# The projection's 101 scratch stores begun by GpSimd instead of the sync engine, in a one-core decoder layer

## The chip, the cores and the metric

The kernel runs on one core of a Trainium2 chip. The metric is the device time of one execution in microseconds; before the change it is 1848.69 us, the median of three runs (1846.27 to 1848.75). Profiled executions are shown in us from the start of the span. The engines are TensorE (PE, and PEld for its weight loads), VectorE (DVE), ScalarE (ACT), GpSimd (POOL) and the sync engine (SP), which computes nothing and begins DMAs.

## The reference, cut to what matters

One layer of a hybrid decoder is computed for a prompt of 2048 tokens and for a group of 8 x 8 sample tokens with the same weights. A normalised input `h` is projected once, and the columns of the projection feed four mixers and a gate:

```
h = rms_norm(x, norm_pre)
proj = jnp.einsum('btd,de->bte', h, w_in)
q = proj[..., OFF_AQ:OFF_AK]; k = proj[..., OFF_AK:OFF_AV]; v = proj[..., OFF_AV:OFF_B]
xb = proj[..., OFF_B:OFF_C]; pc = proj[..., OFF_C:OFF_D]; u = proj[..., OFF_D:OFF_G]; gate = proj[..., OFF_G:]
...
oa = attend(q, k, v, lam)                  # differential attention: w = p0 - lam * p1; w @ v
ob, new_h = rglru(xc, lru_h, ...)          # from xb
oc, new_shift, new_S = rwkv7_mix(pc, ...)
od, new_ssm = s5_mix(u, ...)
o = jnp.concatenate([oa, ob, oc, od], axis=-1) * jax.nn.silu(gate)
y = x + rms_norm(jnp.einsum('bte,ed->btd', o, w_out), norm_post)
```

The change concerns `pc` (the RWKV group's five projections), `u` (the S5 group's) and `gate`, which the kernel computes while it runs the prompt's attention.

## The kernel before

`w_in` is 28 column blocks of 128; a group `g` is two of them. The first stage (to 286 us of the span) normalises the input and projects groups 0 to 3: queries, keys, values and the input of the RG-LRU group, which it also runs. The second stage, 286 to 1008 us, is the one that the change touches. Two lists of work run in it together:

- `attn_prompt` and `attn_rows` (L317, L350): for each of 4 heads and 16 blocks of 128 queries, a row of attention over pieces of 512 keys; 64 rows, 160 pieces. Per piece: the scores `s` (L363, TensorE), their maxima `a_mx` (L367, VectorE), the exponentials `a_e` (L371, ScalarE). Per row, the factors `a_al` (L376 or L387, VectorE). Then per piece the second half of `a_e` is scaled on GpSimd (L391), both halves are joined on VectorE (L392), cast to fp16 as the first half of `a_w` on ScalarE (L395), the remainder of the cast is written as the second half of `a_w` on GpSimd (L396), the sync engine begins a DMA transpose of `a_w` into `a_wt` (L399), and TensorE multiplies `a_wt` by the values into `pv` (L403, L404). `a_w` and `a_wt` have four buffers each.
- `proj_rest` (L583): the 10 other groups of the projection (`FILL`), each 2 column blocks x 5 blocks of tokens (four of 512 and one of 64), 100 accumulations `acc` of 24 matmuls (L206). Each `acc` is evicted into `pst` (three buffers) by ScalarE and VectorE: for `pc` by L624, L626 and L631, for the gate `sg` by L640 to L642, for `u` by L606 on ScalarE alone. Then `pst` is stored to scratch in DRAM: `pc` at L634 (50 stores), `sg` at L643 (40), `u` at L608 (10), and once `shift` at L636. A store of 512 columns is 128 rows of 2 KB; one of `u` is 128 x 8 runs (64 elements each, 8 in the short block). Later stages read `pc`, `u` and `sg`.

The paced order (`paced`, L1783) ties the projection's matmuls to anchors in the attention, so that both lists end together. In the same stage the output weights are halved into fp16 pairs (`w`, L1501 to L1503) and stored (L1504), and the sync engine loads `kh` and `qh` (L330, L335).

The order on each engine is made by the framework's scheduler when the program is built. On the chip each engine and each queue works in that order: an instruction that waits for a semaphore holds up all that stand behind it on its engine. The sync engine's list in this stage is the 160 transposes, the 101 stores, the loads of `kh` and `qh` and the weights' stores.

The last stage, from 1008 us, holds the sample group's attention, S5, RWKV and the output projection.

Of the kernel before, what the change touches and what calls it, by code (L numbers as in the profile page):

```python
# [53 lines left out]
class Part:  # L54
# [528 lines left out]
    def proj_rest(self, groups, wpool, pool, psum, after, aside=iter(())):  # L583


        nc = self.nc
        st_q = nc.sync
        for g in groups:
            for m in range(2):
                w16, un = self.load_w(2 * g + m, wpool)  # L590
# [1391 lines left out]
```

## Time and profile before

| | us |
|---|---|
| median of three runs | 1848.69 |
| the profiled execution | 1857.33 |
| its span | 1855.5 |
| first stage, 0 to 286 | 286 |
| second stage, 286 to 1008 | 722 |
| the rest | 847.5 |
| TensorE busy in the span | 1505.9 (81%) |
| VectorE busy | 1415.4 (76%) |
| ScalarE busy | 902.6 (49%) |
| GpSimd busy | 717.9 (39%) |

The span runs from the first to the last instruction of the program; the profiled execution's own time is 1.8 us longer. The busy time of an engine is that of its instructions alone; a DMA that the sync engine begins is not counted as busy, while one that GpSimd begins stands among its instructions. A wait is put down to the instruction whose semaphore came last. Shares of busy time are averages over stages with different limits, so the table of stretches is read beside them.

### The profile page before, as it was taken

How to read it: one execution, taken by the hardware profiler on the slowest of the kernel's cores; microseconds unless marked ns; L12 is line 12 of the kernel's file. 1: busy time of each engine (PE TensorE's matmuls, PEld its weight loads, DVE VectorE, ACT ScalarE, POOL GpSimd, SP SyncE). 2: the span in 40 equal slices, each digit the busy share in tenths (PEclk: the TensorE clock that was granted, in tenths of full speed). 3: DMA queues.
4: the chain of work that ended last, by engine and by line, in shares of the span. 5: the costliest groups of instructions: out<-in, count | busy, mean ns of one | idle time of the engine just before them, and what ended most of it. 6: DMA issues, size and time to landing. Idle time of an engine off the chain costs nothing.

```text
span 1855.5 us, 32909 instructions
## 1 busy us (share of the span) xinstructions
PE 1505.9 (81%) x10956; PEld 846.6 (46%) x10956; DVE 1415.4 (76%) x4439; ACT 902.6 (49%) x2211; POOL 717.9 (39%) x807
## 2 busy tenths in 40 slices
PE   5889878788878878888895799856777978888887
PEld 2445644344434434444442355545544544544443
DVE  7797638867888897898786765367787886988975
ACT  3445645555655665666773222243334444444443
POOL 3441312343434553563444444253323433334322
PEclk9999998899989998999897798966687878889889
DMA  4422134655545655473445986655223333233221
GB/s 148 128 87 92 35 109 109 151 117 128 110 117 132 140 150 129 115 162 94 86 105 139 270 268 204 193 170 165 75 66 85 106 90 105 82 91 96 65 85 59
DMA packets 300894, 225.31 MB, mean 121 GB/s; under 512 B 192530, under 2 KB 248564, under 8 KB 300212
## 3 DMA queue, kind: packets, MB, share of 16 engines
q1 hardware_dynamic: 288388, 184.85, 37.5%
q10 hardware_dynamic: 8496, 24.76, 4.6%
q0 software_dynamic: 3840, 13.61, 2.7%
q8 instruction: 86, 1.41, 0.3%
q14 instruction: 84, 0.69, 0.1%
HBM read 130.04 MB, written 53.24 MB: 99 GB/s over the span
## 4 chain that ended last, share of the span: by engine, by line
DVE 29%; PE 18%; DMA 14%; issue 12%; POOL 8%; ACT 4%; SPq 1%; ACTq 0%; POOLq 0%; DVEq 0%
DMA r_zr<-zd 6%; PE acc L206 4%; POOL a_w L396 4%; PE acc L1585 4%; POOL a_e L391 3%; DVE a_mx L367 3%; DMA a_wt<-a_w 2%; DVE a_e L392 2%; DVE r_x16w L1263 2%; DVE r_x L1264 2%; PE ss L512 2%; DMA zd<-r_de 2%; DMA kv<-in_ckv 1%; DVE r_W L1178 1%; ACT a_e L371 1%
## 5 line engine op out<-in xcount | busy, mean ns | idle before, releaser
L206 PE MATMUL acc<-hT,w 128*128 128x512 f16 (+1 forms) x3120 | 636.1, 356 | 39.1 <-DVE shf L628 11.9
L206 PEld LDWEIGHTS <-w 128*128 128x128 f16 x3120 | 271.1, 101 | 341.6 <-issue 70.7
L371 ACT ACTIVATE a_e<-s,a_mx,sig 128x512 f32<-128x512 f32 (+3 forms) x320 | 225.3, 713 | 111.0 <-DVE a_mx L368 88.5
L1585 PE MATMUL acc<-wo,o_h 128*128 128x512 f16 (+1 forms) x816 | 226.6, 424 | 3.5 <-DVE o_h L1563 2.1
L391 POOL TENSOR_SCALAR a_e<-a_e,a_al 128x512 f32<-128x512 f32 (+3 forms) x160 | 115.0, 734 | 287.2 <-DVE a_al L387 232.4
L396 POOL TENSOR_TENSOR a_w<-a_e,a_w 128x512 f16<-128x512 f32 (+3 forms) x160 | 180.2, 1142 | 105.0 <-ACT a_w L395 104.9
L367 DVE TENSOR_REDUCE a_mx<-s 128x1 f32<-128x512 f32 (+3 forms) x320 | 184.2, 601 | 30.7 <-PE s L363 16.5
L392 DVE SCALAR_TENSOR_TENSOR a_e<-a_e,a_al 128x512 f32<-128x512 f32 (+3 forms) x160 | 138.5, 884 | 14.4 <-POOL a_e L391 14.2
L363 PE MATMUL s<-kh,qh 128*128 128x512 f16 (+3 forms) x320 | 101.0, 358 | 40.6 <-ACT a_e L371 36.1
L1585 PEld LDWEIGHTS <-o_h 128*128 128x128 f16 (+1 forms) x816 | 77.5, 106 | 99.4 <-issue 29.3
L403 PE MATMUL pv<-vtok,a_wt 128*128 128x128 f16 x544 | 68.9, 229 | 63.7 <-DMA a_wt<-a_w 52.6
L395 ACT CAST a_w<-a_e 128x512 f16<-128x512 f32 (+3 forms) x160 | 85.7, 558 | 63.6 <-DVE a_e L392 61.9
L1263 DVE TENSOR_TENSOR r_x16w<-r_zr,r_x 128x60 f32<-128x60 f32 (+18 forms) x255 | 59.3, 233 | 54.7 <-DMA r_zr<-zd 51.8
L403 PEld LDWEIGHTS <-a_wt 128*128 128x128 f16 x544 | 51.4, 102 | 88.1 <-DMA a_wt<-a_w 76.3
L1600 POOL TENSOR_TENSOR o_x<-o_y,o_x 128x512 f32<-128x512 f32 (+1 forms) x33 | 48.9, 1496 | 105.6 <-DVE o_y L1598 72.5
L170 POOL TENSOR_TENSOR hT<-hf,hT 128x512 f16<-128x512 f32 (+1 forms) x36 | 36.7, 1026 | 88.5 <-ACT hT L168 86.1
L404 PE MATMUL pv<-vtok,a_wt 128*128 128x64 f16 x544 | 64.9, 200 | 0.0
L371 ACT ACTIVATION_READ_ACCUMULATOR a_e<-s,a_mx,sig 128x1 f32 x320 | 64.2, 201 | 0.0
L1264 DVE TENSOR_TENSOR r_x<-r_x,r_x16w 128x60 f32<-128x60 f32 (+18 forms) x255 | 59.9, 235 | 2.9
L512 PE MATMUL ss<-kv,qbd 128*32 128x256 f32 x256 | 52.7, 415 | 7.9 <-DMA kv<-in_ckv 7.9
L368 DVE TENSOR_SCALAR a_mx<-a_mx,sig 128x2 f32<-128x2 f32 x160 | 58.0, 369 | 0.5
L1365 POOL TENSOR_TENSOR r_sd<-r_Z,r_Dp 64x128 f32<-64x128 f32 x64 | 30.1, 470 | 70.0 <-DVE r_Z L1373 63.5
(545 smaller groups left out, 3201.7 us busy)
## 6 DMA issues: line engine op xcount, KB each, us to landing
kv<-in_ckv SPq DMA_DIRECT2D x128, 256.0 KB
w<-in_w_in ACTq DMA_DIRECT2D x20, 512.0 KB
pc<-pst SPq DMA_DIRECT2D x40, 256.0 KB
xw<-in_xT SPq DMA_DIRECT2D x16, 512.0 KB
w<-in_w_out ACTq DMA_DIRECT2D x16, 512.0 KB
sg<-pst SPq DMA_DIRECT2D x32, 256.0 KB
r_X<-pc SPq DMA_DIRECT2D x16, 512.0 KB
r_zr<-zd SPq DMA_DIRECT2D x16, 512.0 KB
```

The costliest lines, as they stand in the source:

```text
L206: self.nc.tensor.matmul(acc[:, :n], w16[:, k, a, :], h[:, k, e, :], start=(c == 0), stop=(c == 3 * KT - 1))
L363: ins = nc.tensor.matmul(s[:, :kn], q[:, c], kh[:, c, k0:k0 + kn], start=True, stop=True)
L367: nc.vector.tensor_reduce(mx[:, p, c:c + 1], s[:, :kn], axis=AX.X, op=ALU.max, negate=True)
L371: nc.scalar.activation(e[:, :kn], s[:, :kn], AF.Exp, scale=sig, bias=mx[:, p, c:c + 1], accum_out=l[:, p, c:c + 1])
L391: nc.gpsimd.tensor_scalar(e1[:, :kn], e1[:, :kn], al[:, p, 1:2], 0.0, op0=ALU.mult, op1=ALU.add)
L392: nc.vector.scalar_tensor_tensor(e0[:, :kn], e0[:, :kn], al[:, p, 0:1], e1[:, :kn], op0=ALU.mult, op1=ALU.add)
L396: nc.gpsimd.tensor_tensor(w[:, kn:], e0[:, :kn], w[:, :kn], op=ALU.subtract)
L403: ins = nc.tensor.matmul(pv[:, :P], wt[:, j], v, start=kt == 0, stop=kt == qb, skip_group_check=True)
L512: ins = nc.tensor.matmul(sp[g:g + 32, 256 * j:min(256 * j + 256, n)], self.qbd[:, m, s].rearrange("p a q -> p (a q)"), rhs, start=True, st ...
L1263: XV.tensor_tensor(w[:, :, :m], zr[:, k, :, k + 1:], x[:, :, k:k + 1].to_broadcast([P, nu, m]), op=ALU.mult)
L1264: XV.tensor_tensor(x[:, :, k + 1:], x[:, :, k + 1:], w[:, :, :m], op=ALU.add)
L1585: nc.tensor.matmul(a[:n].rearrange("p (c n) -> p c n", c=4), h[:, k, e], self.wo[:, 4 * g:4 * g + 4, k, f, :], start=c == 0, stop=c == 3 * ...
```

## The change

The queue that begins the stores of `proj_rest` is GpSimd's instead of the sync engine's. All three store lines and the one of `shift` use it, 101 DMAs. Nothing else in the source changes; where the instructions stand is drawn anew by the scheduler.

```diff
@@ -584,7 +584,7 @@ proj_rest
         nc = self.nc
-        st_q = nc.sync
+        st_q = nc.gpsimd
         for g in groups:
```

On the sync engine, at some 540 us of the span, the stores of three `pst` stood between transposes. `a_wt` is the transpose of the `a_w` that is named behind the arrow. Before:

```order
L399 DMA_TRANSPOSE a_wt_4851<-a_w_4848 128x8x128
L634 DMA pc_1197<-pst_9632 128x512
L399 DMA_TRANSPOSE a_wt_4922<-a_w_4919 128x8x128
L634 DMA pc_1197<-pst_9664 128x512
L634 DMA pc_1197<-pst_9695 128x64
L399 DMA_TRANSPOSE a_wt_4937<-a_w_4934 128x8x128
L399 DMA_TRANSPOSE a_wt_4952<-a_w_4949 128x2x128
```

And now:

```order
L399 DMA_TRANSPOSE a_wt_4851<-a_w_4848 128x8x128
L399 DMA_TRANSPOSE a_wt_4922<-a_w_4919 128x8x128
L399 DMA_TRANSPOSE a_wt_4937<-a_w_4934 128x8x128
L1504 DMA wod_8487<-w16_9913 128x2048
L399 DMA_TRANSPOSE a_wt_4952<-a_w_4949 128x2x128
```

The three stores are gone from this queue; the order of the transposes is kept.

On GpSimd at the same place, `a_w` of a piece and the scaling of the next row's `a_e` stood with only the weights' steps (`w32`, `w16`) between them. Before:

```order
L396 TENSOR_TENSOR a_w_4848<-a_e_4817,a_w_4848 128x512
L391 TENSOR_SCALAR a_e_4881<-a_e_4881,a_al_4871 128x512
L391 TENSOR_SCALAR a_e_4892<-a_e_4892,a_al_4871 128x512
L391 TENSOR_SCALAR a_e_4905<-a_e_4905,a_al_4871 128x128
L396 TENSOR_TENSOR a_w_4919<-a_e_4879,a_w_4919 128x512
L1502 TENSOR_SCALAR w32_9911<-w32_9911,wun_8489 128x1024
L396 TENSOR_TENSOR a_w_4934<-a_e_4890,a_w_4934 128x512
L396 TENSOR_TENSOR a_w_4949<-a_e_4903,a_w_4949 128x128
L1503 TENSOR_TENSOR w16_9913<-w32_9911,w16_9913 128x8x128
L391 TENSOR_SCALAR a_e_4973<-a_e_4973,a_al_4963 128x512
```

And now:

```order
L396 TENSOR_TENSOR a_w_4848<-a_e_4817,a_w_4848 128x512
L634 DMA pc_1197<-pst_9632 128x512
L391 TENSOR_SCALAR a_e_4881<-a_e_4881,a_al_4871 128x512
L391 TENSOR_SCALAR a_e_4892<-a_e_4892,a_al_4871 128x512
L391 TENSOR_SCALAR a_e_4905<-a_e_4905,a_al_4871 128x128
L1502 TENSOR_SCALAR w32_9911<-w32_9911,wun_8489 128x1024
L396 TENSOR_TENSOR a_w_4919<-a_e_4879,a_w_4919 128x512
L396 TENSOR_TENSOR a_w_4934<-a_e_4890,a_w_4934 128x512
L634 DMA pc_1197<-pst_9664 128x512
L1503 TENSOR_TENSOR w16_9913<-w32_9911,w16_9913 128x8x128
L396 TENSOR_TENSOR a_w_4949<-a_e_4903,a_w_4949 128x128
L634 DMA pc_1197<-pst_9695 128x64
```

One store stands straight before a row's `a_e`, one between two `a_w` of the same row, and one after them; a weights' step has moved in front of `a_w_4919`.

On VectorE, which writes both the `a_e` that `a_w_4949` reads and the `pst` that stands ahead of it on GpSimd, the order is now (`a_e_4903` is joined at L392, `pst_9664` is complete with L631):

```order
L392 SCALAR_TENSOR_TENSOR a_e_4903<-a_e_4903,a_al_4871,a_e_4905 128x128
L368 TENSOR_SCALAR a_mx_4961<-a_mx_4961,sig_603 128x2
L367 TENSOR_REDUCE a_mx_5070<-s_5073 128x1
L367 TENSOR_REDUCE a_mx_5070<-s_5076 128x1
L428 TENSOR_SCALAR sl_v_5053<-sl_v_5053 128x8
L626 SCALAR_TENSOR_TENSOR pst_9664<-acc_9639,wsc_9541,pst_9664 128x511
L628 TENSOR_SCALAR shf_1192<-acc_9639,un_9532 128x1
L380 TENSOR_REDUCE a_mm_4999<-a_mx_4961 128x2
L631 SCALAR_TENSOR_TENSOR pst_9664<-plast_9633,vec_74,pst_9664 128x1
```

The last write of `pst_9664` comes eight instructions after `a_e_4903`; on GpSimd its store comes before the `a_w` that reads that `a_e`. Over the stage, 51 of the 101 stores stand straight before an `a_e` (L391), 38 before an `a_w` (L396) and 12 before a weights' step; stores that follow each other are counted with what comes after them.

## Rows read from the trace of the kernel before

**Rows 1.** Table of stretches: length, busy time (instructions) by engine, clock, DMA share, GB/s

```profile
286.00:1008.00 722.00, 603.34 (x3986) 306.04 (x3984) 583.46 (x1536) 440.96 (x1082) 322.13 (x336) 0.93 0.53 122
```

**Rows 2.** The page's chain that ended last: shares of the span by engine, by line

```profile
DVE 29%; PE 18%; DMA 14%; issue 12%; POOL 8%; ACT 4%; SPq 1%; ACTq 0%; POOLq 0%; DVEq 0%
DMA r_zr<-zd 6%; PE acc L206 4%; POOL a_w L396 4%; PE acc L1585 4%; POOL a_e L391 3%; DVE a_mx L367 3%; DMA a_wt<-a_w 2%; DVE a_e L392 2%; DVE r_x16w L1263 2%; DVE r_x L1264 2%; PE ss L512 2%; DMA zd<-r_de 2%; DMA kv<-in_ckv 1%; DVE r_W L1178 1%; ACT a_e L371 1%
```

**Rows 3.** Waits in 286 to 1008: us in total, times, longest us

```profile
POOL a_e L391 <- DVE a_al L387: 232.4, 40, 12.4
POOL a_w L396 <- ACT a_w L395: 104.9, 69, 4.9
...
PE pv L403 <- DMA a_wt<-a_w: 52.6, 38, 8.5
```

**Rows 4.** The sync engine's own waits in 286 to 1008

```profile
SPq L399 <- POOL a_w L396: 218.3, 82, 9.8
SPq L634 <- DVE pst L631: 66.1, 24, 6.3
SPq L643 <- DVE pst L642: 49.0, 14, 10.6
```

**Rows 5.** Tiles `pst` and `a_wt` (last row): duration ns min/median/max, first and last start

```profile
L634 SPq DMA_DIRECT2D pc<-pst x50: 319/338/1108, 299.4 to 722.6; - x50
...
L642 DVE SCALAR_TENSOR_TENSOR pst<-pth,pst x40: 207/682/1644, 732.6 to 997.7; 128x512 f32<-128x512 f32 x32, 128x64 f32<-128x64 f32 x8
...
L631 DVE SCALAR_TENSOR_TENSOR pst<-shi,vec,pst x10: 219/400/2165, 318.2 to 721.5; 128x8 f32<-128x8 f32 x10
...
L399 SPq DMA_TRANSPOSE a_wt<-a_w x160: 1167/1239/3051, 286.2 to 1003.5; - x160
```

**Rows 6.** Timeline of the sync engine, three places: start, us, line, operation, xcount

```profile
357.57 0.32 SPq L634 DMA_DIRECT2D pc<-pst  x1
358.00 2.64 SPq L399 DMA_TRANSPOSE a_wt<-a_w  x2
...
538.47 2.84 SPq L634 DMA_DIRECT2D pc<-pst  x2
541.41 2.59 SPq L399 DMA_TRANSPOSE a_wt<-a_w  x2
...
995.73 3.53 SPq L643 DMA_DIRECT2D sg<-pst  x2
999.36 2.62 SPq L399 DMA_TRANSPOSE a_wt<-a_w  x2
```

**Rows 7.** Timeline of GpSimd, at four places

```profile
262.59 0.54 POOL L743 DMA_DIRECT2D od<-lx  x1 [3.20 <-DVE lru_last L742]
...
355.36 1.56 POOL L396 TENSOR_TENSOR a_w<-a_e,a_w 128x512 f16<-128x512 f32 x2 [0.39 <-ACT a_w L395]
...
537.27 1.54 POOL L396 TENSOR_TENSOR a_w<-a_e,a_w 128x512 f16<-128x512 f32 x2
538.78 2.12 POOL L1503 TENSOR_TENSOR w<-w,w 128x1024 f16<-128x1024 f32 x1
...
997.25 4.25 POOL L396 TENSOR_TENSOR a_w<-a_e,a_w 128x512 f16<-128x512 f32 x3
```

**Rows 8.** Timeline of TensorE: the wait for the second transpose at 541

```profile
546.54 0.23 PE L403 MATMUL pv<-vtok,a_wt 128*128 128x128 f16 x1 [0.83 <-DMA a_wt<-a_w]
```

**Rows 9.** Timeline of VectorE beside two GpSimd instructions

```profile
262.86 0.69 DVE L727 SCALAR_TENSOR_TENSOR lxc<-lt,lxc 128x512 f32<-128x512 f32 x1 [0.38 <-ACT lt L720]
...
538.76 2.17 DVE L631 SCALAR_TENSOR_TENSOR pst<-shi,vec,pst 128x8 f32<-128x8 f32 x1
```

**Rows 10.** Groups of GpSimd: DMAs of 2x128 and 4x128 runs, busy us, mean ns

```profile
L1054 POOL DMA_DIRECT2D s5gy<-yd x8 | 5.9, 738 | 6.3 <-issue 4.2 <-PE x L1064 1.0 <-PE ra L44 1.0
...
L936 POOL DMA_DIRECT2D s5T<-kd x4 | 4.5, 1118 | 0.0
```

**Rows 11.** DMA issues: count, KB each, median us from issue to landing

```profile
od<-lx POOLq DMA_DIRECT2D x2, 256.0 KB, 2.3
```

## The prediction

> **What bounds the kernel now.** I read the table of stages first, then the chain of waits, then who waited for whom inside the stage that the change touches, and last the sync engine's own waits and its timeline beside GpSimd's. The change lives in one stage, 286 to 1008 us of the span, in which attention on the prompt and the projection's other groups run together. In its 722 us TensorE is busy 603, VectorE 583, ScalarE 441 and GpSimd 322 [rows 1]: nothing is full, so the stage is paced by who waits for whom. In the chain of waits GpSimd's `a_w` (L396) and `a_e` (L391) hold 4% and 3%, the transposes' landing (`a_wt<-a_w`) 2% [rows 2]: together 9% of 1855 us, some 165 us, nearly all of it in this stage. That is the loop which the change touches: `a_al` (VectorE), `a_e` (GpSimd), `a_e` again (VectorE), cast (ScalarE), `a_w` (GpSimd), transpose (sync engine), `pv` (TensorE).
>
> At TensorE this loop is seen as 52.6 us of waiting for transposes, in 38 waits [rows 3]. There are 160 transposes, so 38 of 160, or 24%, are what TensorE stands still for; the others come before it asks. I use 0.24 as the **path factor**: what one us of lateness of a transpose costs the stage.
>
> GpSimd in turn waits 232.4 us in 40 waits for `a_al` and 104.9 us in 69 for the cast [rows 3]. It has 400 us of idle time, but in two kinds: long waits before `a_e` (5.8 us each) and short ones before `a_w` (1.5 us each).
>
> The sync engine waits 218.3 us in 82 waits at the transposes for `a_w` [rows 4]: for at least 82 of 160 transposes it stood ready and GpSimd was late. It also waits 66.1 and 49.0 us (24 and 14 times) at the stores for VectorE's last write of `pst` [rows 4]. Those are the waits that leave its queue.
>
> **The change, part by part.** 101 DMAs (90 stores of `pc` and `sg`, 10 of `u`, one of `shift`) leave the sync engine and are begun by GpSimd. On the sync engine a store costs 0.34 us and a transpose 1.24 [rows 5], so some 34 us of issue go, beside some 200 us of transposes that stay. The issue time alone is worth little; what counts is the transposes that stood behind a store.
>
> *What the sync engine gains.* I took the 160 transposes one by one from the two timelines: the time from the end of its `a_w` to its issue, and how much of that passed in a store or in the wait before it. 23 are late for a store, by 28.1 us in all. First: a pair of `a_w` done at 356.92, a store at 357.57, the transpose at 358.00. Largest: a pair of `a_w` done at 538.81, two stores from 538.47 to 541.31, the pair of transposes begun at 541.41. Last: three `a_w` from 997.25, two stores that hold the queue until 999.26, the transpose at 999.36 [rows 6, 7]. Even the largest costs TensorE only 0.83 us, at 546.54 [rows 8], a third or less of its lateness, which agrees with the factor. Gain: 28.1 x 0.24 = **-6.7 us**. Bounds: 0 (TensorE waits for `a_w` anyway) and -28.1 (every us of it reaches the end).
>
> *What GpSimd pays for the issue.* A store of 128 rows of 2 KB took GpSimd 0.54 us (`od<-lx` at 262.59 [rows 7]). The `u` stores go out in 128 x 8 runs, which no GpSimd row shows; 2 x 128 runs took 0.74 us and 4 x 128 took 1.12 [rows 10], or 0.19 us more for each 128, so 8 x 128 is an estimate of 1.9 us (bounds 1.12 and, at twice the step, 2.6). In sum 91 x 0.54 + 10 x 1.9 = 68 us on an engine that was busy 322 of 722 us. Where they stand decides. In the new order 51 stand straight before an `a_e`, 38 before an `a_w`, 12 before the output weights' steps. The 51 cost nothing: GpSimd waits there for `a_al` (5.8 us a wait), and in VectorE's new order every such `a_al` comes after the `pst` of the store ahead of it, so the store is out before its `a_e` could start. That cover is gone if `a_al` follows `pst` by under 0.54 us. The 12 delay weights that are needed only after the stage. The 38 push `a_w`: 34 x 0.54 + 4 x 1.9 = 26 us, times 0.24 = **+6.2 us** (bounds 0 and 68).
>
> *What GpSimd pays in waiting.* GpSimd works its queue in order, so an `a_w` whose data are there waits behind a store whose `pst` isn't. The order shows 30 such places of 160, where the last write of `pst` stands on VectorE one to nine instructions after the `a_e` that this `a_w` reads; `a_w_4949` behind `pst_9664`, shown above, is one. Queued behind it are this `a_w`, its transpose, and the next row's `a_e`. No row of before shows the length of such a wait on GpSimd; the nearest is the same encounter on the sync engine, 28.1 us in 23, or 1.2 each. 30 x 1.2 x 0.24 = **+8.8 us**. Bounds: 0 (the cast covers it) and 115 x 0.24 = 28 us, if GpSimd inherits the whole wait at the two larger store lines [rows 4].
>
> *Hidden.* `pst` has three buffers and a store that GpSimd began landed 2.3 us after its issue [rows 11], while a new `pst` is made every 7.2 us (722 / 100); the reuse of `pst` stays covered, unless GpSimd is some 12 us behind. The DMA engines are 53% busy in the stage [rows 1] and move the same bytes.
>
> *Later stages.* Rows after 1008 us are also drawn in another order, with the same instructions. I take 0 and widen the range by 4 us on either side.
>
> **Sum:** -6.7 + 6.2 + 8.8 = +8.3 us. The profiled execution took 1857.3 us (span 1855.5 and 1.8 around it), 8.6 above the median 1848.7, so a profile like it would read 1865.6, and the median 1857.0.
>
> **A rule about the shared port.** At 538.76 a VectorE instruction on 128x8 elements took 2.17 us, while GpSimd worked on `w` (L1503) from 538.78 to 540.90 [rows 7, 9]; the median of that line is 0.40 [rows 5]. So a GpSimd instruction can hold VectorE up. While GpSimd issued a DMA from 262.59, a 128x512 VectorE instruction with two SBUF inputs took 0.69 us [rows 7, 9], as long as the same form at L642 (median 0.68 [rows 5]). The Trainium skill (SBUF — State Buffer, Who interferes with whom) says that the two engines share one pair of ports, which is locked for a whole instruction, and that writing the descriptors of a GpSimd DMA needs it too. By the first row it is right; by the second an issue does not hold VectorE up. What it would cost is the fourth rival.
>
> **The rivals.**
> 1. *Faster: the sync engine is freed and GpSimd's idle time takes the rest.* For it: 400 us of idle time, and 51 of the stores stand in its long waits. Against it: 38 don't. It gives -6.7, or 1842.0 us; to the bound of -28 it is 1821. Chance 0.25.
> 2. *No difference.* The transposes wait for `a_w` (82 waits) and the few us either way cancel: 1848.7 within 3.7 us, which is 0.2% and about what a measurement of this kernel can tell from no change. The Trainium skill (DMA: Bandwidth & Descriptors, Issuing engines are not separate DMA queues) speaks for this one: it says that another issuing engine saves its sequencer's time alone. Chance 0.25.
> 3. *GpSimd becomes the gate: clearly slower.* The projection's pace is laid on the attention loop at its tightest engine: GpSimd stands at a store, `a_e` of the next row comes late, then its transpose, then `pv`. Price: the full 28 us of waiting and 68 x 0.24 = 16 of issue, less 6.7: +37, or 1886 us. It decides from the point where GpSimd's waits at stores pass some 60 us. Chance 0.09.
> 4. *The port.* If each issue held VectorE for its length, 68 us would fall on an engine that is busy 81% of the stage: 55 us, of which VectorE's share of the chain, 29% [rows 2], is 16; with the sum, +24, or 1873 us. The row at 262.59 speaks against it. Chance 0.05.
>
> **How the numbers follow.** My forecast, slower by some 8 us (own range 1852.5 to 1870), has 0.36. Slower by over 0.2%: 0.36 + 0.09 + 0.05 = 0.50. Within 0.2%: 0.25. Faster: 0.25. For 8 in 10 I go up to 1877, which leaves out most of rival 3 (0.09), and down to 1839, which takes in rival 1 at its price and leaves out its far end (some 0.10).
>
> **What would show it.** In the profile after: the sync engine has no waits but at transposes and loads, and its lateness behind stores is gone; GpSimd has 101 more DMAs, `u` at about 1.9 us each and the rest at 0.54, and is busy some 390 us in the stage; `a_w` (L396) waits more often, with a store just ahead of it; TensorE's wait for `a_wt` is above 52.6 us. I am wrong in the path if GpSimd's waits grow and TensorE's don't, wrong in size if the stage is longer by over 25 us, and wrong in sign if TensorE waits under 46 us for transposes and the stage is shorter.

## The result, and the profile after

The changed kernel took **1865.53 us** (three runs, 1864.89 to 1866.35) against 1848.69: a ratio of 1.0087, 95% interval 1.0067 to 1.0107. It is slower by 16.8 us. (In the runs below the kernel before had medians of 1849.7 to 1851.5 us; against these the loss is 14 to 16 us.) I had forecast 1857.0, so the direction held and the size was half of what came. The runs below show that it came by another working than mine.

The stage of the change, in the table of stretches, as [rows 1], and the chain of waits, as [rows 2]:

```profile
286.00:1008.00 722.00, 599.23 (x3952) 302.37 (x3951) 603.45 (x1533) 439.09 (x1077) 374.84 (x429) 0.94 0.52 120
```

```profile
DVE 35%; PE 18%; DMA 13%; issue 9%; ACT 6%; POOL 5%; SPq 0%; ACTq 0%; POOLq 0%; DVEq 0%
DMA r_zr<-zd 6%; PE acc L206 5%; DVE a_mx L367 4%; DVE a_e L392 4%; PE acc L1585 3%; ACT a_e L371 2%; DVE r_x16w L1263 2%; DVE r_x L1264 2%; POOL a_e L391 2%; PE ss L512 2%; DMA zd<-r_de 2%; DMA a_wt<-a_w 2%; DVE a_mx L368 2%; POOL a_w L396 1%; DVE r_W L1178 1%
```

In the same 722 us TensorE did 3952 of the 3986 matmuls and GpSimd was busy 53 us longer. The stage now ends with its last `pv` at 1017.9 us of the span; before it was 1007.4. In the chain GpSimd's share fell from 8% to 5% and VectorE's rose from 29% to 35%.

The waits of that stage (286 to 1018: us, times, longest), as [rows 3], the sync engine's own, as [rows 4], and the stores and transposes, as [rows 5] (ns, shortest/median/longest):

```profile
POOL a_e L391 <- DVE a_al L387: 81.0, 34, 5.7
POOL a_w L396 <- ACT a_w L395: 64.6, 54, 4.5
PE pv L403 <- DMA a_wt<-a_w: 49.0, 32, 6.2
PE s L363 <- ACT a_e L371: 36.1, 34, 5.2
```

```profile
SPq L399 <- POOL a_w L396: 446.9, 106, 15.5
```

```profile
L634 POOL DMA_DIRECT2D pc<-pst x50: 540/590/600, 299.9 to 732.6; - x50
L643 POOL DMA_DIRECT2D sg<-pst x40: 541/589/591, 739.4 to 1010.0; - x40
L608 POOL DMA_DIRECT2D u<-pst x10: 886/924/964, 366.4 to 429.9; - x10
L399 SPq DMA_TRANSPOSE a_wt<-a_w x160: 1167/1233/2974, 285.4 to 1013.7; - x160
```

GpSimd's groups in the stage (busy us, mean ns | idle before them, by what):

```profile
L634 POOL DMA_DIRECT2D pc<-pst x50 | 28.7, 574 | 81.4 <-issue 35.7 <-ACT a_e L371 10.5 <-DVE a_mm L384 7.3
L643 POOL DMA_DIRECT2D sg<-pst x40 | 22.9, 574 | 60.8 <-DVE a_mx L368 20.0 <-DVE pst L642 19.4 <-DVE a_mm L384 7.6
L608 POOL DMA_DIRECT2D u<-pst x10 | 9.2, 920 | 20.9 <-ACT a_t L408 11.2 <-ACT pst L606 9.8
```

The sync engine does what was foreseen: no wait for a store is left, and it stands at the transposes for `a_w`, 446.9 us in 106 waits. GpSimd waits 163 us at the stores, and 151 us less before `a_e`: most of its waiting has only moved from the `a_e` to the store that now stands ahead of it. And TensorE's wait for transposes, on which my sum rested, did not grow: 49.0 us against 52.6. Its wait at the scores for ScalarE's exponentials (`PE s L363`) did, from 26.9 us to 36.1. So the cost isn't to be seen where I looked for it, when the two profiles are held against each other. They also hold two different orders, which is what the experiments take apart.

### The profile page after: what moved, and what is told of

Read it like the earlier page. It is cut to its first block, busy times and chain, and to the rows that moved or that the text cites. A ratio compares the mean times of both kernels' runs of the same rounds, so it can differ in the third digit from the quotient of the medians.

```text
span 1863.7 us, 32930 instructions
## 1 busy us (share of the span) xinstructions
PE 1501.0 (81%) x10956; PEld 843.5 (45%) x10956; DVE 1426.6 (77%) x4439; ACT 903.7 (48%) x2211; POOL 773.0 (41%) x908
## 4 chain that ended last, share of the span: by engine, by line
DVE 35%; PE 18%; DMA 13%; issue 9%; ACT 6%; POOL 5%; SPq 0%; ACTq 0%; POOLq 0%; DVEq 0%
DMA r_zr<-zd 6%; PE acc L206 5%; DVE a_mx L367 4%; DVE a_e L392 4%; PE acc L1585 3%; ACT a_e L371 2%; DVE r_x16w L1263 2%; DVE r_x L1264 2%; POOL a_e L391 2%; PE ss L512 2%; DMA zd<-r_de 2%; DMA a_wt<-a_w 2%; DVE a_mx L368 2%; POOL a_w L396 1%; DVE r_W L1178 1%
## 5 line engine op out<-in xcount | busy, mean ns | idle before, releaser
L1585 PE MATMUL acc<-wo,o_h 128*128 128x512 f16 (+1 forms) x816 | 218.8, 413 | 5.0 <-DVE o_h L1563 2.3
L396 POOL TENSOR_TENSOR a_w<-a_e,a_w 128x512 f16<-128x512 f32 (+3 forms) x160 | 176.0, 1116 | 66.2 <-ACT a_w L395 64.6
L391 POOL TENSOR_SCALAR a_e<-a_e,a_al 128x512 f32<-128x512 f32 (+3 forms) x160 | 119.7, 759 | 120.1 <-DVE a_al L387 81.0
L392 DVE SCALAR_TENSOR_TENSOR a_e<-a_e,a_al 128x512 f32<-128x512 f32 (+3 forms) x160 | 149.9, 956 | 17.2 <-POOL a_e L391 17.2
L363 PE MATMUL s<-kh,qh 128*128 128x512 f16 (+3 forms) x320 | 103.7, 363 | 46.6 <-ACT a_e L371 45.2
L368 DVE TENSOR_SCALAR a_mx<-a_mx,sig 128x2 f32<-128x2 f32 x160 | 66.1, 421 | 0.4
L634 POOL DMA_DIRECT2D pc<-pst x50 | 28.7, 574 | 81.4 <-issue 35.7
```

Of the source, the lines that this page charges most:

```text
L363: ins = nc.tensor.matmul(s[:, :kn], q[:, c], kh[:, c, k0:k0 + kn], start=True, stop=True)
L368: nc.vector.tensor_scalar(mx[:, p], mx[:, p], sig, None, op0=ALU.mult)
L391: nc.gpsimd.tensor_scalar(e1[:, :kn], e1[:, :kn], al[:, p, 1:2], 0.0, op0=ALU.mult, op1=ALU.add)
L392: nc.vector.scalar_tensor_tensor(e0[:, :kn], e0[:, :kn], al[:, p, 0:1], e1[:, :kn], op0=ALU.mult, op1=ALU.add)
L396: nc.gpsimd.tensor_tensor(w[:, kn:], e0[:, :kn], w[:, :kn], op=ALU.subtract)
L1585: nc.tensor.matmul(a[:n].rearrange("p (c n) -> p c n", c=4), h[:, k, e], self.wo[:, 4 * g:4 * g + 4, k, f, :], start=c == 0, stop=c == 3 * ...
```

## The experiments

**Parts of the change.** Three kernels move one kind of store each, as this one does, and a fourth gives all of them to ScalarE:

```diff
-        st_q = nc.sync
...
-                        st_q.dma_start(self.u[m, :, :, c0:c0 + n // TS].rearrange("l p c -> p l c"),
+                        nc.gpsimd.dma_start(self.u[m, :, :, c0:c0 + n // TS].rearrange("l p c -> p l c"),
```

> Only the 10 stores of u (L608) are begun by GpSimd; pc and sg stay on the sync engine. In this order 9 of the 10 stand before an a_e (L391) and one before an a_w (L396). Theory 1 (a store costs what it holds up of a_w, in issue and in waiting for pst): 10 x 0.92 us of issue, nearly all of it in GpSimd's long waits, so no difference, 1846 to 1852 us. Theory 2 (the redrawn order sets the time, not the stores): any value from 1840 to 1866, without relation to the number of stores moved.

1.0050 (1.0020 to 1.0080), 1858 us: a small loss where theory 1 had none; theory 2 allowed any value up to 1866.

> Only the 50 stores of pc and the one of shift are begun by GpSimd. In this order 18 of them stand straight before an a_w, 10 of these with a pst that VectorE finishes after the a_e which that a_w reads. Theory 1: about half of what the whole change costs (16.8 us by the medians), so 1854 to 1860 us. Theory 2 (redrawn order): the parts do not add up to the whole; one of pc alone and sg alone lies within 2 us of the kernel before or under it, or costs as much as the whole. Theory 3 (VectorE is held longer by a_w because the two now meet more often): L368 and L392 rise on VectorE as they did with the whole change (369 to 421 ns and 884 to 956 ns in the mean) whichever part is moved.

1.0221 (1.0173 to 1.0269), 1889 us, more than the whole change. Theory 3 has its mark here: L368 takes 422 ns in the mean and L392 935.

> Only the 40 stores of sg are begun by GpSimd. 17 stand straight before an a_w, 11 of them with an unready pst. Theory 1: about half of the whole, 1854 to 1860 us, and all of it after 722 us of the span. Theory 2: no such sum, see pc alone. Theory 3: L368 and L392 longer only after 722 us.

1.0141 (1.0094 to 1.0188), 1875 us. Here L368 did not rise (360 ns), while L392 did (932).

The parts cost 9, 40 and 26 us by their medians against the 1849.7 of before: 74 us in sum, where the whole costs 17. No sum of stores gives that. Theory 1, as I had stated it, falls here. The third part says where to look. In the run with `sg` alone the stage ended at 1007.6 us as before, and all of its loss lies behind it, where no store is begun.

```diff
-        st_q = nc.sync
+        st_q = nc.scalar
```

> All 101 stores are begun by ScalarE, at 0.34 us each as its loads of w are (L177). The sync engine is relieved as in the change, and GpSimd begins none of them. My term for the sync engine (23 transposes late behind stores, 28.1 us x 0.24) then stands nearly alone: 1842 us, plus up to 34 x 0.24 = 8 us if ScalarE's exponentials and casts pay for the issue. If the change's loss came from the sync engine's new order and not from GpSimd, this run shows the same loss, 1860 or more.

1.0012 (0.9990 to 1.0033): no difference. With the sync engine relieved and GpSimd left alone nothing is gained, nor lost, in an order that was drawn anew here too.

**Order and queue apart.** Each edit lets the planner draw a new order. So I wrote an order of instructions into the kernel: one list for each engine, taken from a built program, whose neighbours are tied by edges that fix the order and add no wait. Where a run moves the 101 stores (or the 40 of `sg`) to another queue, these are left out of the table and the planner places them, but for the run with six buffers of `pst`.

```diff
         program(tc, ins, outs)
+        keep_order(nc, tc)
...
+def keep_order(nc, tc):
+    traced = list(nc.cur_bb.bb.instructions)
+    for rows in ORDER.values():
...
+            if last is not None and i.engine == last.engine:
+                tc.add_manual_dep(i, last.name, mybir.DependencyInfo(mybir.DependencyClass.NoSync,
+                                  mybir.DependencyReason.DATA), reason="order")
+            last = i
```

> The kernel before, with its order of instructions on all five engines written into it as a table: nothing differs from before. It is the control of the table and a second profile of the same program. Expected by every theory: 1848.7 us within 4, and the stage from 286 us ending within 2 us of 1007.4.

0.9983 (0.9954 to 1.0012): as before. Its stage ended at 1000.8 us, not within 2 us of 1007.4 as I had expected, and its profiled execution had a span of 1837.5 us where that of before had 1855.5, with the same order; so two profiles of one program can differ by 18 us, and below both stand as the reference.

> The order of the kernel before on all five engines, held by the same table, with the 101 stores alone moved to GpSimd's queue (29 of them straight before an a_w, 17 with an unready pst, 58 before an a_e). Theory 1 (what the stores hold up on GpSimd is the cost): the stage is longer by 5 to 14 us and the time 1854 to 1864. Theory 2 (the redrawn order is the cost): as before, 1848.7 within 4 us. If the sync engine's relief is worth my 6.7 us and the rest nothing: 1842.

With this beside the table:

```diff
-        st_q = nc.sync
+        st_q = nc.gpsimd
```

1.0137 (1.0088 to 1.0186), 1873 us against 1851.5, above what either theory had: **in this order the queue alone costs at least as much as the whole change** (22 to 25 us against 16.8; the two intervals overlap).

> The reverse: the order of the changed kernel on all five engines, with the 101 stores back on the sync engine. Theory 1: 1844 to 1852 us, no slower than before. Theory 2: as the changed kernel, 1862 to 1868 us, the stage ending near 1018 us.

The table is the changed kernel's, the stores are back on `nc.sync`. 1.0035 (1.0010 to 1.0060), 1857 us, between the two theories: **the new order alone costs some 6.5 us**, 0.35% of 1851.5 (2 to 11 by the interval).

| order of | stores on the sync engine | stores on GpSimd |
|---|---|---|
| the kernel before | 1 (control 0.9983) | 1.0137 |
| the changed kernel | 1.0035 | 1.0087 |

GpSimd's queue costs 1.4% in the order that wasn't drawn for it, and 1.0087 / 1.0035 = 0.5%, some 10 us, in the order that was (4 to 16 us by the two intervals, and the two numbers come from different chips).

> The order of the run with sg alone moved, on all five engines, with its 40 stores back on the sync engine. That run was 26 us slower than before, and all of it after 1008 us, where no store is begun. Theory 2: 1868 to 1880 us again, with the whole loss after 1008 us. Theory 1: 1846 to 1852 us.

1.0091 (1.0064 to 1.0117), 1866 us: close under theory 2, so by the ratio this order alone costs 12 to 22 us. In this pair the rest of the kernel after the stage, with its stores on GpSimd and back on the sync engine, then the same stretch in the control (us, length, then busy time of TensorE, its weight loads, VectorE, ScalarE, GpSimd, clock, DMA share, GB/s):

```profile
1008.00:1876.00 868.00, 679.73 (x5286) 409.07 (x5286) 623.29 (x2291) 313.31 (x863) 307.06 (x383) 0.81 0.42 125
```

```profile
1000.00:1856.00 856.00, 675.25 (x5286) 406.56 (x5286) 623.43 (x2290) 313.69 (x863) 307.70 (x383) 0.82 0.42 127
```

```profile
1001.00:1837.00 836.00, 667.62 (x5286) 401.78 (x5286) 628.09 (x2291) 314.52 (x864) 310.43 (x384) 0.83 0.43 130
```

The same 5286 matmuls take 856 us with the stores back on the sync engine, against 836 and, in the profile of before, 848. The stage of the change ended no later than in the control (999.3 us against 1000.8), so what this order costs, it costs in stages where nothing was edited. How much, these single profiles tell to some 12 us only, by which the two of one order differ.

**What it is that GpSimd's queue costs.** All three hold the order of before.

```diff
-                    st = pool.tile([P, 512], F32, name="pst", bufs=3)
+                    st = pool.tile([P, 512], F32, name="pst", bufs=6)
```

(and in GpSimd's list each store that stood before an `a_w` is moved on, to the next `a_e`)

> The order of the kernel before on all engines, the 101 stores on GpSimd, but none of them in front of an a_w: the 29 that stood there in the run with the held order are put off to the next a_e or later (85 before an a_e, 16 elsewhere), with six buffers for pst, since they now go out later. If stores in front of an a_w are the whole cost and the sync engine's relief is worth my 6.7 us: 1843. If the relief is worth nothing: 1850 within 4. If stores in front of an a_e cost as well (GpSimd's long waits do not cover them): 1858 or more.

1.0102 (1.0069 to 1.0136), 1869.6 us. Not one store stands before an `a_w`, and most of the loss is still there. My account of the cost, that only stores which push `a_w` cost anything, falls with this run, and so does the price of nothing that I gave the stores before an `a_e`. (The six buffers were not tried by themselves.)

```diff
+        dum = self.dram.tile([128, P, 1], F32, name="dum")
...
+                    self.dums.append(nc.gpsimd.dma_start(dum[len(self.dums)], self.sub8).ins.name)
                     yield
```

> The order of the kernel before on all engines, the stores on the sync engine as before, and at the 100 places where GpSimd begins a store in the run with the held order it begins a small transfer instead (128 runs of 4 bytes, from a constant): the issue without the wait for pst. With 29 of them before an a_w at about 0.57 us, 17 us. With my path factor 0.24: 4 us, 1854. With a factor of 1, as the first run with the held order suggests: 1867. If GpSimd's waiting for pst is the cost and not the issue: 1850 within 3.

1.1752, 2173 us. This run tells nothing about the issue: the small transfer wasn't small. GpSimd's queue moved 0.05 MB more, and with that the other transfers took longer. The two queues of section 3 that the edit doesn't touch, with the same packets and bytes, in the control:

```profile
q1 hardware_dynamic: 288388, 184.85, 37.6%
q10 hardware_dynamic: 8496, 24.76, 4.6%
```

and with the 100 transfers:

```profile
q1 hardware_dynamic: 288388, 184.85, 42.1%
q10 hardware_dynamic: 8496, 24.76, 7.6%
q0 software_dynamic: 7040, 13.66, 2.4%
```

The shares are of a span that was itself 18% longer, so the packets of ScalarE's queue (q10, most of them loads of weights) took 1.9 times as long. TensorE's wait for transposes rose from 49.2 us to

```profile
PE pv L403 <- DMA a_wt<-a_w: 296.7, 68, 14.2
```

> As the last, but 80 of the small transfers stand straight before every second a_w of the 160 and 20 after the last one: a measurement of the path factor. 80 x 0.57 = 46 us of GpSimd's time in front of a_w. Factor 0.24: +11 us, 1861. Factor 1: +46, 1896. If GpSimd's waits for the cast cover the issue: 1850 to 1855.

1.1818, 2186 us, with the same sign (q10 at 7.4% of a span of 2178 us); the path factor stays unmeasured.

```diff
-        st_q = nc.sync
+        st_q = nc.scalar
```

> The order of the kernel before on all engines, held by the table, with the 101 stores begun by ScalarE (0.34 us each by its loads of w): the sync engine is relieved as in the change, GpSimd begins none of them. It measures the sync engine's relief alone, and the difference to the run with the held order and the stores on GpSimd is what GpSimd pays. My term for the relief: -6.7 us, 1843. If the relief at TensorE's waits is as large as in the run on GpSimd (15 us of steps by earlier transposes): 1835. If ScalarE pays for the issue (16 stores stand before a cast, 40 before an exponential) or the relief is hidden: 1848 to 1853, no difference. If a second queue for the stores is what makes the transposes land late, whichever engine begins them: 1860 or more.

1.0006 (0.9982 to 1.0030), with the order of before held. So the relief of the sync engine, a second queue for the stores and what ScalarE pays for 101 issues together don't move the time. GpSimd as the engine that begins them does.

**Where the time goes.** The stage from 286 us to its last `pv`, the same matmuls in each: the profile of before, the control, the stores on ScalarE, on GpSimd, on GpSimd but not before an `a_w` (all five in one order), and then the changed kernel's order with the stores on the sync engine and on GpSimd:

```profile
286.00:1007.00 721.00, 602.95 (x3984) 305.86 (x3983) 583.23 (x1535) 440.65 (x1081) 321.26 (x334) 0.93 0.53 122
```

```profile
286.00:1001.00 715.00, 596.65 (x3984) 303.75 (x3983) 581.84 (x1534) 439.93 (x1080) 319.74 (x334) 0.94 0.53 123
```

```profile
286.00:1013.00 727.00, 604.55 (x3988) 305.59 (x3986) 585.25 (x1535) 441.11 (x1084) 321.50 (x336) 0.93 0.54 121
```

```profile
286.00:1027.00 741.00, 611.89 (x3984) 309.64 (x3982) 598.51 (x1534) 440.43 (x1080) 377.56 (x436) 0.91 0.52 119
```

```profile
286.00:1026.00 740.00, 613.13 (x3980) 310.75 (x3980) 590.34 (x1530) 440.29 (x1079) 379.80 (x435) 0.91 0.53 119
```

```profile
286.00:1010.00 724.00, 602.12 (x3987) 305.02 (x3985) 590.47 (x1535) 440.75 (x1084) 327.26 (x336) 0.94 0.53 122
```

```profile
286.00:1018.00 732.00, 602.51 (x3984) 304.81 (x3983) 606.03 (x1534) 440.76 (x1080) 380.02 (x435) 0.93 0.53 120
```

Length less TensorE's busy time is what TensorE stood idle: 118.1 and 118.4 us in the two references, 129.1 and 126.9 with the stores on GpSimd in the order of before. That is 9 to 11 us. The rest of the 19 to 26 us by which the stage grew is busy time: the same matmuls took 9 to 16 us longer, at a mean granted clock of 0.91 instead of 0.93 and 0.94. In the changed kernel's own order the idle time went from 121.9 to 129.5 us and the busy time stayed. These are single profiles, and some us of them are chance: with the stores on ScalarE the stage has 122.5 us of idle time and is 6 to 12 us longer, while that kernel's time is level with before.

The clock has two levels, 2.4 and 1.2 GHz. In these stages the lower one was granted for 100 and 87 us in the two references and 99 us with the stores on ScalarE, but for 133 and 126 us with them on GpSimd in the order of before. In the changed order it was 92 us with the stores on the sync engine and 97 on GpSimd.

Two other readings set the runs side by side. The first is TensorE's wait for transposes, in the control, with the stores on ScalarE, on GpSimd, and on GpSimd but not before an `a_w`:

```profile
PE pv L403 <- DMA a_wt<-a_w: 49.2, 32, 8.4
```

```profile
PE pv L403 <- DMA a_wt<-a_w: 62.4, 42, 7.9
```

```profile
PE pv L403 <- DMA a_wt<-a_w: 63.8, 34, 8.5
```

```profile
PE pv L403 <- DMA a_wt<-a_w: 56.1, 36, 8.3
```

It is as long with the stores on ScalarE, where nothing was lost, as with them on GpSimd; so a longer wait for transposes is not by itself the loss. The second is VectorE's busy time in the rows of the stage, and that does go with GpSimd: against the two references it is 2 to 3 us more with the stores on ScalarE (585.25), 7 to 17 us more with them on GpSimd (590.34 and 598.51), and in the changed order 15.6 us more (606.03 against 590.47). That is what theory 3 had, VectorE held longer. No run takes it away alone, so it stands as a rival beside the late transposes and the issues' time on GpSimd.

One place shows a late transpose and the clock together. The timeline of TensorE in the control (start, us, line, operation, xcount, the wait before it):

```profile
433.70 0.22 PE L403 MATMUL pv<-vtok,a_wt 128*128 128x128 f16 x1
...
433.87 2.32 PE L206 MATMUL acc<-hT,w 128*128 128x512 f16 x10
```

and with the stores on GpSimd, not before an `a_w`; then GpSimd just before it, and the stretch that follows as a row of the table of stretches:

```profile
438.15 0.23 PE L403 MATMUL pv<-vtok,a_wt 128*128 128x128 f16 x1 [1.94 <-DMA a_wt<-a_w]
...
438.33 3.88 PE L206 MATMUL acc<-hT,w 128*128 128x512 f16 x10
```

```profile
430.40 0.67 POOL L396 TENSOR_TENSOR a_w<-a_e,a_w 128x256 f16<-128x256 f32 x1 [0.80 <-ACT a_w L395]
431.01 1.82 POOL L608 DMA_DIRECT2D u<-pst  x2
```

```profile
439.00:442.00 3.00, 3.00 (x8) 1.06 (x7) 2.47 (x7) 0.21 (x1) 0.19 (x1) 0.50 0.00 1
```

Up to here that kernel was 2.3 us behind the control. The transpose was issued 2.3 us later as well, right behind its `a_w`, which no store had held up; but its last packet ended 4.1 us after its issue instead of 2.4, and TensorE was released 2.5 us after that, where some 0.6 is the median of such waits. Two stores of `u` that GpSimd had begun were on their way meanwhile, in packets of 4096 and 2048 bytes, most of which took 0.2 to 0.8 us. From 433 to 434 us the queue of the transposes started 53 packets, where it had started 895 in the us before. (At the release a load of weights of ScalarE's was on its way too; which of them held it up isn't shown.) TensorE stood still for 1.94 us. Then the clock was granted at the lower of its two levels (0.50 of 2.4 GHz in 439 to 442, 1.00 in 432 to 438), and the same ten matmuls took 3.88 us, not 2.32. Here a late transpose was paid for twice.

## Why the prediction came out near, and which steps failed

**The sync engine's gain, -6.7 us: it does not show.** The lateness behind stores did vanish: from the end of an `a_w` to the issue of its transpose it is 0.28 us in the mean, where it was 0.62. But both runs with the stores on ScalarE, which relieve the sync engine in the same way, are level with before (1.0012 and 1.0006). They leave room for 3 us of gain at most, unless ScalarE lost by the issues what the sync engine gained. What the transpose gains at its issue is partly lost on its way: in the profiles of the held order, issue to last packet (mean, after 445 us) is 2.75 us in the control, 3.00 with the stores on ScalarE, 2.91 with them on GpSimd and 3.15 with them there but not before an `a_w`.

**The issue, +6.2, and the waiting, +8.8: both too large in us, and priced by a wrong factor.** The prices were good for `pc` and `sg` (0.57 against 0.54) and double for `u` (0.92; I had worked out 1.9 from the steps of [rows 10]). In the changed kernel a store stood between a finished cast and its `a_w` in 26 places, and cost 15.3 us by its issue and 8.4 by its wait; before an `a_e` it was 4.4 us. I had 26 and 36, and 0. So 28 us of direct delay, and not 62.

**The path factor, 0.24, and what it multiplies: this is the step that failed.** I had priced GpSimd's queue as the delay of `a_w` times 0.24. In the order of before, 15.6 us of delay before `a_w` and 4.9 before `a_e` came with a loss of 22 us by the medians and 25 by the ratio, where the factor gives 5. With the stores moved on there was no delay before `a_w` and some 7 us before `a_e`, and the loss was still 19 us. In the changed kernel's order 28 us came with some 10. So no one factor turns this delay into the loss. I had taken mine from the share of transposes that TensorE waits for, which counts who waits now, and not who would wait if they came later. It also left out the clock, which at 438 us made 1.94 us of waiting into 3.5, and it left out the longer instructions on VectorE. How the loss of GpSimd's queue divides among these stays open.

**The stores before `a_e`: not free.** I took 51 stores there at nothing. As delay they were nearly that, 4.4 us in the changed kernel; but with the stores put there on purpose the loss is 1.0%. So they cost more than the time for which they hold their `a_e` up. How much of it is transposes that land late, VectorE held longer or the store's own time on GpSimd, I could not separate, since the small transfers of the runs made for that slowed the other transfers.

**A term that I did not have: the redrawn order itself, 6.5 us.** I knew that all orders were drawn anew and gave it 0, with 4 us on either side for the later stages. In this change the later stages did stay within that (845 us after the stage, 846 and 836 to 848 in the others). In the run with `sg` alone they took 868 us, and 856 in its order with the stores back on the sync engine.

So 0 + some 10 + 6.5 stands where I had -6.7 + 15.0 + 0 (the 10 is what the 16.8 leaves beside the 6.5). This split holds for the changed kernel's order; in the order of before the queue alone is 22 to 25 us. The sign was right since the largest part, GpSimd's queue, has the sign that I gave it; that the sum came within 8.5 us was luck in the parts.

**My marks.** "TensorE's wait for `a_wt` above 52.6" failed against before (49.0) and held in its direction against the same order with the stores on the sync engine, where the wait was 45.0 us. A mark that compares two profiles with different orders was no test, and with 62.4 us and no loss in the run on ScalarE it would be none in one order either. The sync engine's waits, the number of DMAs and GpSimd's busy time (380 us to the stage's end; I had some 390) came as marked. The `u` stores took half of their 1.9 us, and `a_w` did not wait more often for its cast (54 times against 69).

**The rivals.** The first (faster by the sync engine's gain) and the second (no change) are out; the second is what ScalarE as the issuing engine gives. The Trainium skill (DMA: Bandwidth & Descriptors, Issuing engines are not separate DMA queues) has it that DMAs begun on several engines save only the sequencer's time to begin them. With ScalarE no more than that was saved (1.0006), which agrees; with GpSimd the time rose (1.0137), which a saving alone does not give. The third, GpSimd as the gate, priced at 37 us, is nearest in kind to the run with the held order, at 25.

The fourth rival, the port: that each issue holds VectorE for its length is out. Of 75 VectorE instructions of the changed kernel that began in the issue of a store early enough to end in it, 70 did; and the 146 that met an issue of `pc` or `sg` and nothing else on GpSimd lost nothing in sum against the median of their kind. But an issue can hold VectorE up together with what follows it: an L368, 0.22 us when GpSimd is idle, began at 605.84, inside an issue of `pc` (605.76 to 606.37), and ended at 607.59, with the `a_w` behind the issue (606.39 to 607.56). Another 65 instructions met such an issue and a GpSimd instruction beside it, and took some 25 us longer than the median of their kind. So my reading of the row at 262.59, that an issue does not hold VectorE up, was too wide.

VectorE's two groups of the loop in the whole span, before, in the changed order with the stores on the sync engine, and after:

```profile
L392 DVE SCALAR_TENSOR_TENSOR a_e<-a_e,a_al 128x512 f32<-128x512 f32 (+3 forms) x160 | 138.5, 884 | 14.4 <-POOL a_e L391 14.2
L368 DVE TENSOR_SCALAR a_mx<-a_mx,sig 128x2 f32<-128x2 f32 x160 | 58.0, 369 | 0.5
```

```profile
L392 DVE SCALAR_TENSOR_TENSOR a_e<-a_e,a_al 128x512 f32<-128x512 f32 (+3 forms) x160 | 145.2, 927 | 15.1 <-POOL a_e L391 15.1
L368 DVE TENSOR_SCALAR a_mx<-a_mx,sig 128x2 f32<-128x2 f32 x160 | 58.6, 372 | 0.4
```

```profile
L392 DVE SCALAR_TENSOR_TENSOR a_e<-a_e,a_al 128x512 f32<-128x512 f32 (+3 forms) x160 | 149.9, 956 | 17.2 <-POOL a_e L391 17.2
L368 DVE TENSOR_SCALAR a_mx<-a_mx,sig 128x2 f32<-128x2 f32 x160 | 66.1, 421 | 0.4
```

The instructions of L368 that met an `a_w` took 0.65 us in the mean before (44 of them) and 0.95 after (40), against 0.22 when GpSimd was idle. These are 19.5 us more of VectorE's time, 7.3 by the order alone and 12.2 by GpSimd's queue; what of it reached the end wasn't tried.

## What to carry to other kernels

When a planner redraws the order on every edit, first hold the old order and change the queue alone, and then the reverse: two runs split a difference that no comparison of two profiles can. A waiting engine's idle time is no promise of room for more instructions: the same 101 issues cost 1.4% on GpSimd and nothing on ScalarE, and both are steps of the loop that the other engines wait for. A share of "who waits today" is no price for lateness. Where TensorE's granted clock falls after a wait, as at 438 us here, count the wait and the matmuls after it.

## What was unexpected

- GpSimd's stores travel in other packets. Against before, section 3 of the profile after has 23504 packets less in the sync engine's queue and 7072 more in GpSimd's, for the same 21.7 MB; by the packets' sizes in the trace, the stores of 512 columns of `u` go in pieces of 256 bytes from the sync engine and of 4096 from GpSimd, and those of `pc` and `sg` in pieces of 2048 and of 4096.

```profile
q1 hardware_dynamic: 264884, 163.17, 33.7%
q0 software_dynamic: 10912, 35.29, 6.5%
```

- 100 transfers of 128 runs of 4 bytes to DRAM, begun by GpSimd, cost 323 us (2173.3 against 1850.4), 3.2 us each, while the transfers of the other queues took longer. Which part of the path they hold isn't shown.
- The two profiles of the same order differ in the stage by 6 us (721 and 715), and all of it is TensorE's busy time (602.95 and 596.65).
